# Own-key terms of linear attention from one GpSimd product, and narrow TensorE products in groups of one shape

## The chip, the cores and the metric

One core of a Trainium2 chip runs the whole program. The metric is the device time of one execution in microseconds (us); for the kernel before, the median of three runs is 1870.88 us.

## What is computed

Two transformer blocks over 512 tokens of 1024 channels, in float32. The first block is a token mixer with four groups of heads, and a gated feed-forward layer with a convolution; the second has a short-convolution mixer, a latent attention and two more feed-forward layers. The change lies in the token mixer, in two of its four parts:

- The gated delta rule, four heads of 64 channels. Per chunk of 64 tokens it needs `k k^T` and `q k^T` within the chunk, weighted by decays, the inverse of a unit lower triangular matrix, and the products of that inverse with the values (u) and with the decayed keys (w).
- Linear attention with decays per channel, once as `hg` (four heads of 64 key channels) and once as `gla` (four heads of 32):

```python
a_intra = jnp.einsum('bhnrd,bhnsd,bhnrsd->bhnrs', q, k, jnp.exp(rel))   # s <= r within a block
o_intra = jnp.einsum('bhnrs,bhnse->bhnre', a_intra, v)
```

The term of a token with its own key (r = s) has a decay of 1, so it is the sum over the head's channels of q times k.

## The kernel before, in words

Every product of a weight is made of three float32 matmuls with operands split into high and low parts (`product`, `step`): a column tile of the weight (128 columns) times 512 tokens, eight k tiles deep. Activations are kept as [128 channels, 512 tokens].

The mixer is the first phase (`mix`). `conduct` (L757) writes out the order of TensorE's work by hand. Three lanes hold the mixers as generators: G the gated delta (`gdn`, L1035, two calls of two heads), L the linear attention (`hg` twice with two heads a tile, `gla` once with four heads, all through `la`, L1314), F the forgetting attention. A generator yields the time that the operands of its next products are expected to take; a clock summed from modelled product times decides which lane is due. In between, and at the latest after 1.27 us of lanes' work, one k tile (three matmuls) of a dense product goes into the queue. The dense products are the 29 column tiles of the input weight and, at the end, the 8 of the output weight. Only TensorE's order is fixed so; the other engines' order comes from a scheduler that follows the program's order and the readiness of operands.

Each lane has a ring of PSUM tiles of its own, two deep (`gps`, `lps`, `fps`). Short-lived SBUF tiles of lane L come from the ring `s` of four. `mm` (L703) issues one product, which is two instructions on TensorE for float32 operands; `tr` (L710) a transpose.

In `la`, L1320 to L1334, each head has four products of 128x128 (one a chunk of 128 tokens) of the keys with the queries, on the head's 64 or 32 rows. VectorE multiplies the result by the identity (L1333), which leaves the own-key terms on the diagonal of the tile `lat`; all else in the 128x128 blocks is filled in by seven levels (`la_level`, L1289: a subtraction on GpSimd at L1298, exponentials on ScalarE, products on GpSimd at L1302 and VectorE at L1309). Before that, GpSimd clears the tiles `lbd` (L1322).

In `gdn`, L1075 to L1112, a loop over the two heads makes the gates `e` (in TensorE, then ScalarE), yields, multiplies keys by queries on the head's 64 rows (four products), weights them on VectorE (`weighted`, L1026, four instructions a head), yields, multiplies keys by keys, weights those in place of the gates, and makes from them `mr`, `t1` (mask, L1109) and `xt` (plus identity, L1110). After the loop the values and then both `xt` are transposed (L1115, L1120). At L1164 to L1169 the products of the inverse with the values (`up`: 128x128 weight, 64 columns) and of the keys with the inverse (`wp`: weight of 64 columns, 128 columns moving) alternate, sixteen in all.

Of the kernel before, what the change touches and what calls it, by code (L numbers as in the profile page):

```python
# [9 lines left out]
F32 = mybir.dt.float32  # L10
# [5 lines left out]
ALU = mybir.AluOpType  # L16
AX = mybir.AxisListType

S = 512
# [8 lines left out]
class Builder:  # L28
# [22 lines left out]
    def t(self, shape=(128, S), dt=F32, tag="t", bufs=None, name=None):  # L51
        """A short-lived tile; a lane of the mixer has rings of its own."""
        pool = self.tmp
        if tag in self.lane:
            tag, bufs, own = self.lane[tag]
            pool = self.ph if own else pool
        return pool.tile(list(shape), dt, tag=tag, name=name or tag, bufs=self.rings.get(tag, bufs or 1))
# [12 lines left out]
    def mmt(self):  # L70
        """PSUM of a dense product: two tiles that outlive a phase, or three."""
        self.turn += 1
        if self.turn % self.nmm < 2:
            return self.pmm.tile([128, S], F32, tag="mm", name="mm")
        return self.psm.tile([128, S], F32, tag=self.third, name="mm", bufs=2 if self.third == "pt" else 1)
# [13 lines left out]
    def weight(self, w, ct, kt, between=None, eng=None):  # L89
        """One column tile of a weight: exact high and low parts, [128, kt, 128] in pieces."""  # L90
# [23 lines left out]
    def dense(self, w, ct, xs):  # L114
        """PSUM [128 columns, S tokens] = W[:, ct]^T x, xs a list of (high, low) tiles."""
        return self.product(self.weight(w, ct, len(xs)), xs)
# [14 lines left out]
    def rsqrt_wide(self, ps, scale, tag, n=S):  # L131
        """(mean + eps)^-1/2, with a Newton step, of sums ps (times scale) in PSUM [128, S]."""
# [28 lines left out]
    def stats(self, xs, n, tag):  # L161
        """rows of 1/rms of the tokens on every partition, xs a list of [128, S] tiles."""
# [5 lines left out]
    def gained(self, x, g, tag, bufs=KD):  # L168
        """Exact parts of x times its per-partition gain."""
# [15 lines left out]
    def ready(self, i, ks):  # L185
        """The parts of the x in ks that norm i takes."""
        self.nxt += [self.gained(self.x[k], self.gain(i, k), "x") for k in ks]

    def products(self, w, cts):
        """1 / rms of the tokens, and the products of column tiles with the x of ready()."""  # L190
# [17 lines left out]
    def add_to_x(self, w, xs, gi, n=0):  # L208
        """x += W^T xs, and what the next norm takes of it."""
# [9 lines left out]
    def conv(self, z, y, w, b=None):  # L219
        """y[:, t] = sum_j w[:, j] z[:, t + j] (+ b); z has taps-1 leading zero columns."""  # L220
# [38 lines left out]
    def silu(self, out, z, last=True):  # L259
        """z sigmoid(z); the last of a row brings exp and ln back."""  # L260
# [62 lines left out]
    def final(self, w, xs, gi, out):  # L323
        """The last product and the last norm; the last column tile comes in two halves of the
        tokens, so that the norm of the first runs beside the second."""
# [30 lines left out]
    def write(self, out, half, r):  # L356
        """x times r of one half of the tokens, to DRAM by pairs of tiles."""
# [18 lines left out]
def round_magic(nc, out, in0, scale, shift):  # L376
    """out = nearest integer of in0 * scale + shift."""
# [6 lines left out]
class Mla(Builder):  # L384
# [16 lines left out]
    def rope_tables(self):  # L401
        """cos and signed sin [128, S]; row p serves frequency p % 32."""
# [24 lines left out]
    def swapped(self, raw):  # L427
        """The halves of the rotary columns in each other's place."""
# [20 lines left out]
    def latent(self, cs, g, tag):  # L449
        """Tiles normalised over all their columns, in parts."""  # L450
# [17 lines left out]
    def rotated(self, raw, sw):  # L468
        """The parts of two heads' rotary queries: of the first head the high one over the low
        one, of the second the low one over the high one."""  # L470
# [21 lines left out]
    def mla(self, gi_kv, gi):  # L492
# [15 lines left out]
        # v [tokens, columns] in parts  # L508
# [57 lines left out]
    def scores(self, p, h, b, qn, qr, kn):  # L566
        """Softmax of one head's scores for a block of 128 queries, in rows; gives its last steps."""
# [24 lines left out]
    def attend(self, h, p, vs):  # L592
        """Parts of one head's values weighted by p; a generator that stops after each transpose
        of a block of keys, two blocks ahead of the products."""
# [32 lines left out]
# column tiles of w_in  # L627
# [16 lines left out]
# from a product's end to the next one's start over a step of ScalarE, VectorE, GpSimd (us)  # L644
LA, LV, LP = 0.68, 1.0, 1.5
# the lanes' work between two steps of a dense product, which keep TensorE's clock up (us)
FEED = 1.27
# expected waits (us) on which the order of the lanes' work is set: for a lane's last values, a
# forgetting attention's and a gated delta's inputs, the small gates, 1 / rms, a scaled product,
# a row of silus, the last input of the last products  # L650
# [12 lines left out]
class Mix(Mla):  # L663
    """The mixers' short products run in lanes; a lane is a list of generators that yield
    how long the operands of their next products take. In between go dense products."""

    def mix_consts(self):
# [11 lines left out]
        self.nm1, self.negt = m[:, 0:128], m[:, 128:256]  # L679
        self.resets = c.tile([128, S], BF16, name="resets")  # L680
# [33 lines left out]
    def mm4(self, l, r, cols=lambda t: t):  # L714
        """Block by block l^T r, of some columns."""
# [6 lines left out]
    def stepped(self, ws, xs, tag):  # L722
        """dense(), a generator that stops after each k tile; xs: (k tile, high, low), still
        growing. Yields None where the next is not there yet."""
# [13 lines left out]
    def row_of_out(self, i):  # L738
        """Exact parts of rows of w_out: [128, column tile, 128]."""
# [8 lines left out]
    def idle_psum(self, lanes, live):  # L748
        """PSUM of lanes that have come to their end."""
# [3 lines left out]
    def later(self, gen):  # L753
        """Run gen beside the lane's next task."""
        self.beside.append(Strand(gen, self.clk, self.lane))

    def conduct(self, jobs, lanes):  # L757
        """jobs: (column tile of w_in, task that must be over, name, what to do with the
        product), the urgent first; lanes: lists of (names of inputs, name, generator, rings)."""
# [12 lines left out]
        while True:  # L772
            # what the lanes can start on, and what is due
# [6 lines left out]
            # dense products: evacuate, load the next one's weight  # L780
# [88 lines left out]
    def log1pexp(self, out, z, tmp):  # L869
        """out = ln(1 + exp(-|z|))"""  # L870
# [5 lines left out]
    def rsqrt_small(self, v, n, tag):  # L876
        """v^-1/2 with a Newton step, v an SBUF tile [128, n]."""
# [10 lines left out]
    def to_tokens(self, src, n=4):  # L888
        """PSUM [128 tokens, block, 128 columns] of src [128 columns, tokens]."""
# [5 lines left out]
    def scaled(self, dst, after=None, last=None):  # L895
        """What to do with a product of w_in: times 1 / rms of the tokens, into a new tile."""
# [11 lines left out]
    def silus(self, y, name, last):  # L908
        """silu of y in place, in a row with those that wait if it is the last of the row."""
# [31 lines left out]
    def small(self):  # L941
        """The narrow columns: forget, beta and decay logits, low-rank gate."""
# [3 lines left out]
        # gated delta: [tokens, chunk, head]  # L946
# [30 lines left out]
    def small_fox(self):  # L977
        """Rows 0..3 of a tile: minus the running sum of the log forget gates."""
# [9 lines left out]
    def finish(self, op, pair, gate, g, scale, f=None, dst=None):  # L988
        """RMS over each head of o [tokens, block, 2 heads, 64], gain and gate, in columns."""
# [36 lines left out]
    def weighted(self, out, ps, w, j, e):  # L1026
        """out = ps * e times the row weights w of head j."""
# [7 lines left out]
    def gdn(self, p):  # L1035
# [12 lines left out]
        # sums of squares of the heads, per token  # L1048
# [15 lines left out]
        # 1 / |k|^2 and exp of beta's logarithm less or plus decays  # L1064
# [9 lines left out]
        MT, MR, AT, X, XT = [], [], [], [], []  # L1074
        for j in range(2):  # L1075
            rows = slice(64 * j, 64 * j + 64)
# [9 lines left out]
            for c in range(4):  # L1086
# [3 lines left out]
                )  # L1090
            yield Y_GDN / (1 + j)
            kp = self.pst()
            for c in range(4):
                cs = slice(c * 128, c * 128 + 128)
                self.mm(kp[:, cs], k[rows, cs], q[rows, cs])
            at = self.b("gat", bufs=2)
            self.weighted(at, kp, ik, j, e)
            yield LV
            kp = self.pst()
            for c in range(4):  # L1100
                cs = slice(c * 128, c * 128 + 128)
                self.mm(kp[:, cs], k[rows, cs], k[rows, cs])
            mt = e
            self.weighted(mt, kp, ik, j, e)
# [6 lines left out]
            MT.append(mt), MR.append(mr), AT.append(at), XT.append(xt)  # L1111
            yield LV  # L1112
# [33 lines left out]
        # one refinement: X + X (1 - T X), the defect in float32  # L1146
# [13 lines left out]
        # chunk recurrence  # L1160
# [3 lines left out]
        for c in range(4):  # L1164
            for j in range(2):
                cs = slice(c * 128, c * 128 + 128)
                hs = slice(c * 128 + j * 64, c * 128 + j * 64 + 64)
                self.mm(up[:, hs], XT[j][:, cs], vn[:, hs])
                self.mm(wp[64 * j : 64 * j + 64, cs], ke[:, hs], XT[j][:, cs])  # L1169
# [53 lines left out]
    def hg_bounds(self):  # L1223
        """Lower bounds from a softmax over the one layer, and their logarithms."""
# [17 lines left out]
    def hg_gates(self, p):  # L1242
        """From the forget logits: log forget gates in place, and the keys."""

        def after(f):
# [8 lines left out]
            # logaddexp(ln lb, ln(1 - lb) + f)  # L1254
# [34 lines left out]
    def la_level(self, lv, q, k, g128, g16, es, nh):  # L1289
        """Keys and queries of one level, both decayed to the middles of its blocks."""  # L1290
# [12 lines left out]
        # the heads' queries in blocks of columns of their own  # L1303
# [383 lines left out]
```

## Time and profile before

| | |
|---|---|
| runs | 1869.34, 1870.88, 1871.36 us; median 1870.88 |
| span of the profiled execution | 1867.5 us |
| the profiled execution's own time | not among the numbers at hand; its span is 3.4 us below the median |
| TensorE (PE) busy | 1832.4 us, 98% |
| VectorE (DVE) | 1053.4 us, 56% |
| ScalarE (ACT) | 738.6 us, 40% |
| GpSimd (POOL) | 193.9 us, 10% |
| mixers | from 0 to about 400 us |

The span goes from the first to the last instruction that the profiler records; the time of a run also holds what lies around it. Busy time of TensorE counts pipelined matmuls by their full durations, which overlap: what a product costs the queue is read from the start of one to the start of the next. L numbers are lines of the kernel. A tile's name stands for all its buffers: `lps<-lq,lk` is a product into lane L's PSUM of operands `lq` and `lk`.

### The profile page before, as it was taken

To read this page: it belongs to the slowest core of one execution; us is meant where nothing else is said; L and a number is where in the kernel's file an instruction comes from. 1 tells how busy PE (TensorE), PEld (TensorE's weight loads), DVE (VectorE), ACT (ScalarE), POOL (GpSimd) and SP (SyncE) were. 2 spreads that over 40 slices of the span, in tenths; PEclk is the share of its full clock that TensorE was granted. 3 is DMA by queue.
4 is the path that set the end of the run, shared out by engine and by line. 5 is a ranking of instruction groups with operands and counts; after the bars stand their busy time and mean duration, and the time that the engine had idled before them with its cause. 6 is when DMAs were issued, how large, how long until landed. Compare 5 with 4: busy or idle time off the path is not lost.

```text
span 1867.5 us, 22057 instructions
## 1 busy us (share of the span) xinstructions
PE 1832.4 (98%) x8609; PEld 1502.7 (80%) x8609; DVE 1053.4 (56%) x1627; ACT 738.6 (40%) x1138; POOL 193.9 (10%) x225
## 2 busy tenths in 40 slices
PE   8999999999999999999999999999999999999997
PEld 6787887778888888888888888888777888888886
DVE  7875976767777633455564444334866454444323
ACT  6543534554444422322342332323576433232322
POOL 1510502210000000111200000000111200000001
PEclk9999999999999999999999999999999999999999
DMA  4101111322232333222222223332212222222332
GB/s 166 57 35 46 46 35 35 110 96 97 95 102 91 96 94 97 98 102 91 101 96 102 90 102 99 95 93 97 69 51 74 79 91 102 97 95 97 96 93 76
DMA packets 53223, 162.61 MB, mean 87 GB/s; under 512 B 6528, under 2 KB 13184, under 8 KB 53120
## 3 DMA queue, kind: packets, MB, share of 16 engines
q1 hardware_dynamic: 52992, 161.21, 26.1%
q8 instruction: 67, 1.10, 0.2%
q14 instruction: 36, 0.29, 0.1%
q10 hardware_dynamic: 128, 0.01, 0.0%
HBM read 157.78 MB, written 2.10 MB: 86 GB/s over the span
## 4 chain that ended last, share of the span: by engine, by line
PE 88%; DVE 7%; ACT 2%; issue 1%; POOL 1%; DMA 0%; DVEq 0%; SPq 0%; POOLq 0%; ACTq 0%
PE mm L125 24%; PE mm L127 24%; PE mm L126 24%; PE mm L704 6%; PE gps L704 3%; PE ps L576 2%; PE lps L704 1%; PE fps L704 1%; DVE lbd L1309 1%; DVE lat L1360 1%; DVE wl L112 1%; ACT wh L111 1%; PE pt L605 0%; PE ps L165 0%; POOL s L1298 0%
## 5 line engine op out<-in xcount | busy, mean ns | idle before, releaser
L111 ACT ACTIVATE wh<-raw 128x1024 fp32r<-128x1024 f32 (+3 forms) x308 | 308.7, 1003 | 763.0 <-PE mm L126 463.6
L125 PE MATMUL mm<-xh,wh 128*128 128x512 f32 x1336 | 522.2, 391 | 0.5 <-ACT xh L173 0.5
L126 PE MATMUL mm<-xl,wh 128*128 128x512 f32 x1336 | 521.1, 390 | 0.5 <-DVE xl L174 0.5
L127 PE MATMUL mm<-xh,wl 128*128 128x512 f32 x1336 | 520.3, 389 | 0.0
L112 DVE TENSOR_TENSOR wl<-raw,wh 128x1024 fp32r<-128x1024 f32 (+3 forms) x300 | 362.5, 1208 | 224.7 <-ACT wh L111 221.6
L126 PEld LDWEIGHTS mm<-xl,wh 128*128 128x128 f32 x1336 | 250.9, 188 | 54.5 <-DVE xl L174 1.4
L125 PEld LDWEIGHTS mm<-xh,wh 128*128 128x128 f32 x1336 | 250.9, 188 | 53.6 <-issue 1.0
L127 PEld LDWEIGHTS mm<-xh,wl 128*128 128x128 f32 x1336 | 250.9, 188 | 52.2 <-issue 0.2
L125 PE MATMUL mm<-hidh,wh 128*128 128x512 f32 (+1 forms) x614 | 236.9, 386 | 0.0
L127 PE MATMUL mm<-hidh,wl 128*128 128x512 f32 (+1 forms) x614 | 235.4, 384 | 0.0
L126 PE MATMUL mm<-hidl,wh 128*128 128x512 f32 (+1 forms) x614 | 234.0, 381 | 0.0
L127 PEld LDWEIGHTS mm<-hidh,wl 128*128 128x128 f32 x614 | 115.4, 188 | 24.3
L704 PE MATMUL mm<-xh,wh 128*128 128x512 f32 x291 | 127.7, 439 | 6.8 <-ACT xh L173 5.9
L126 PEld LDWEIGHTS mm<-hidl,wh 128*128 128x128 f32 x614 | 115.5, 188 | 23.4
L125 PEld LDWEIGHTS mm<-hidh,wh 128*128 128x128 f32 x614 | 115.7, 188 | 21.7 <-ACT wh L111 0.2
L704 PE MATMUL mm<-xh,wl 128*128 128x512 f32 x291 | 116.2, 399 | 1.7 <-DVE wl L112 1.7
L704 PE MATMUL mm<-xl,wh 128*128 128x512 f32 x291 | 116.4, 400 | 0.6 <-DVE xl L112 0.4
L278 DVE TENSOR_TENSOR u<-mm,rb 128x512 f32<-128x512 f32 x44 | 30.4, 692 | 141.2 <-PE mm L127 141.2
L158 POOL TENSOR_TENSOR z<-z,sq 128x512 f32<-128x512 f32 x31 | 50.3, 1624 | 558.8 <-ACT sq L156 521.1
L274 DVE TENSOR_TENSOR u<-mm,rb 128x512 f32<-128x512 f32 x44 | 30.4, 691 | 90.9 <-PE mm L127 90.8
L111 ACT ACTIVATE hidh<-s 128x512 fp32r<-128x512 f32 x66 | 41.7, 632 | 88.6 <-DVE s L255 57.5
L704 PEld LDWEIGHTS mm<-xh,wh 128*128 128x128 f32 x291 | 56.1, 193 | 18.8 <-ACT xh L173 6.6
(434 smaller groups left out, 2095.5 us busy)
## 6 DMA issues: line engine op xcount, KB each, us to landing
raw<-in_w_a_dram SPq DMA_DIRECT2D x52, 512.0 KB, 3.3
raw<-in_w_b_dram SPq DMA_DIRECT2D x52, 512.0 KB, 3.3
raw<-in_w_up_dram SPq DMA_DIRECT2D x44, 512.0 KB, 3.2
raw<-in_w_in_dram SPq DMA_DIRECT2D x28, 512.0 KB, 3.2
raw<-in_conv_w_in_dram SPq DMA_DIRECT2D x24, 512.0 KB, 3.2
raw<-in_w_down_dram SPq DMA_DIRECT2D x16, 448.0 KB, 3.2
raw<-in_w_a_dram SPq DMA_DIRECT2D x16, 448.0 KB, 3.3
raw<-in_w_b_dram SPq DMA_DIRECT2D x16, 448.0 KB, 3.3
```

The source lines that it names most:

```text
L111: nc.scalar.activation(out=h, in_=src, func=ACTF.Copy)
L112: (eng or nc.vector).tensor_tensor(out=l, in0=src, in1=h.bitcast(F32), op=ALU.subtract)
L125: nc.tensor.matmul(out=ps, lhsT=h, rhs=xh, start=(k == 0), stop=False)
L126: nc.tensor.matmul(out=ps, lhsT=h, rhs=xl, start=False, stop=False)
L127: nc.tensor.matmul(out=ps, lhsT=l, rhs=xh, start=False, stop=(k == kt - 1))
L158: eng.tensor_tensor(out=acc, in0=acc, in1=sq, op=ALU.add)
L274: nc.vector.tensor_tensor(out=g, in0=ps, in1=r, op=ALU.mult)
L278: nc.vector.tensor_tensor(out=g, in0=ps, in1=r, op=ALU.mult)
L576: nc.tensor.matmul(out=ps[:, :n], lhsT=l[:, qs], rhs=r[:, :n], start=(i == 0), stop=False)
L704: self.nc.tensor.matmul(out=out, lhsT=lhsT, rhs=rhs, start=start, stop=stop)
L1309: nc.vector.tensor_tensor(out=bd[rows, :, h].rearrange("p c (n j) -> p c n j", j=b), in0=c4(q)[rows], in1=c4(d)[rows], op=ALU.mult)
L1360: nc.vector.copy_predicated(out=at.rearrange("p c (n j) -> p c n j", j=2 * b)[:, :, :, b:], mask=self.lmask[:, lv - 1].rearrange("p (n j) ...
```

## The change

In the constants, one column of ones per head:

```diff
+        self.heads = {}
+        for nh in (2, 4):
+            self.heads[nh] = c.tile([128, nh], F32, name=f"heads{nh}")
+            nc.vector.tensor_reduce(
+                out=self.heads[nh], in_=self.ident.rearrange("p (h d) -> p h d", h=nh), axis=AX.X, op=ALU.add
+            )
```

In `la`, queries times keys are formed once on GpSimd, and four products with the head columns (weight: 128 channels by 128 tokens; moving: 2 or 4 columns) sum them over each head's channels. VectorE multiplies the identity by the column of sums:

```diff
+        own = self.t(tag="s", bufs=3)
+        nc.gpsimd.tensor_tensor(out=own, in0=q, in1=k, op=ALU.mult)
+        yield LP
+        kp = self.pst()
+        for c in range(4):
+            self.mm(kp[:, c * nh : c * nh + nh], own[:, c * 128 : c * 128 + 128], self.heads[nh])
+        kp = kp[:, : 4 * nh].rearrange("p (c h) -> p c h", h=nh)
         for h in range(nh):
-            rows = slice(h * dk, h * dk + dk)
-            yield LV
-            kp = self.pst()
-            for c in range(4):
-                cs = slice(c * 128, c * 128 + 128)
-                self.mm(kp[:, cs], k[rows, cs], q[rows, cs])
             at = self.b("lat", bufs=4)
-            nc.vector.tensor_tensor(out=c4(at), in0=c4(kp), in1=idb, op=ALU.mult)
+            nc.vector.tensor_tensor(
+                out=c4(at), in0=idb, in1=kp[:, :, h].unsqueeze(2).to_broadcast([128, 4, 128]), op=ALU.mult
+            )
             AT.append(at)
```

In `gdn`, the gates of both heads come first, then both heads' keys with queries in one group that alternates between the heads' rows, then both heads' keys with keys:

```diff
+            E.append(e)
             yield Y_GDN / (1 + j)
-            kp = self.pst()
+
+        def keys_with(r):
+            kp = [self.pst() for _ in range(2)]
             for c in range(4):
                 cs = slice(c * 128, c * 128 + 128)
-                self.mm(kp[:, cs], k[rows, cs], q[rows, cs])
+                for j in range(2):
+                    rows = slice(64 * j, 64 * j + 64)
+                    self.mm(kp[j][:, cs], k[rows, cs], r[rows, cs])
+            return kp
+
+        for j, kp in enumerate(keys_with(q)):
             at = self.b("gat", bufs=2)
-            self.weighted(at, kp, ik, j, e)
-            yield LV
-            kp = self.pst()
-            for c in range(4):
-                cs = slice(c * 128, c * 128 + 128)
-                self.mm(kp[:, cs], k[rows, cs], k[rows, cs])
-            mt = e
-            self.weighted(mt, kp, ik, j, e)
+            self.weighted(at, kp, ik, j, E[j])
+            AT.append(at)
+        yield 2 * LV
+        for j, kp in enumerate(keys_with(k)):
+            mt = E[j]
+            self.weighted(mt, kp, ik, j, mt)
             mr = self.b("gmr", F32R, bufs=2)
...
-            MT.append(mt), MR.append(mr), AT.append(at), XT.append(xt)
-            yield LV
+            MT.append(mt), MR.append(mr), XT.append(xt)
+        yield LV
```

and the products with the inverse are issued as all of `up`, then all of `wp`:

```diff
-        for c in range(4):
-            for j in range(2):
-                cs = slice(c * 128, c * 128 + 128)
-                hs = slice(c * 128 + j * 64, c * 128 + j * 64 + 64)
-                self.mm(up[:, hs], XT[j][:, cs], vn[:, hs])
-                self.mm(wp[64 * j : 64 * j + 64, cs], ke[:, hs], XT[j][:, cs])
+        blocks = [
+            (slice(c * 128, c * 128 + 128), slice(c * 128 + j * 64, c * 128 + j * 64 + 64), j)
+            for c in range(4) for j in range(2)
+        ]
+        for cs, hs, j in blocks:
+            self.mm(up[:, hs], XT[j][:, cs], vn[:, hs])
+        for cs, hs, j in blocks:
+            self.mm(wp[64 * j : 64 * j + 64, cs], ke[:, hs], XT[j][:, cs])
```

The constants on which `conduct` sets the order (LA, LV, LP, Y_GDN and the others) stay. The diff also drops comments, which changes no instruction.

## Rows read from the trace of the kernel before

**Rows 1.** The page: its first line, and the busy time of TensorE.
```profile
span 1867.5 us, 22057 instructions
...
PE 1832.4 (98%) x8609; PEld 1502.7 (80%) x8609; DVE 1053.4 (56%) x1627; ACT 738.6 (40%) x1138; POOL 193.9 (10%) x225
```

**Rows 2.** Busy time by stretch: length, each engine (instructions), clock, DMA share, GB/s.
```profile
175.00:200.00 25.00, 24.75 (x122) 18.94 (x121) 19.01 (x33) 12.24 (x23) 7.05 (x6) 1.00 0.18 64
200.00:225.00 25.00, 24.81 (x135) 20.05 (x134) 22.40 (x62) 16.69 (x38) 13.21 (x12) 1.00 0.12 43
225.00:250.00 25.00, 23.55 (x137) 20.10 (x135) 21.77 (x62) 7.14 (x8) 5.43 (x6) 1.00 0.13 43
...
0.00:400.00 400.00, 378.45 (x2094) 310.74 (x2094) 294.31 (x629) 194.63 (x380) 98.38 (x110) 0.99 0.20 68
```

**Rows 3.** Timeline of TensorE about one narrow group of gdn: start us, us, instruction.
```profile
57.76 0.39 PE L704 MATMUL mm<-xh,wl 128*128 128x512 f32 x1
58.08 1.16 PE L704 MATMUL gps<-gq,gk 64*128 64x128 f32 x8
...
59.50 0.39 PE L704 MATMUL mm<-xl,wh 128*128 128x512 f32 x1
59.73 0.40 PE L704 MATMUL mm<-xh,wl 128*128 128x512 f32 x1
```

**Rows 4.** Instructions of line 704, the narrow groups: min/median/max ns, first and last start.
```profile
L704 PE MATMUL lps<-lq,lk x64: 269/272/374, 65.9 to 321.7; 64*128 64x128 f32 x32, 32*128 32x128 f32 x32
...
L704 PE MATMUL gps<-gq,gk x32: 271/272/374, 58.1 to 220.6; 64*128 64x128 f32 x32
```

**Rows 5.** Timeline of TensorE about products with 16 columns, in the small gates.
```profile
33.27 0.29 PE L704 MATMUL gps<-gg,mixc 128*128 128x16 f32 x2
33.40 0.38 PE L704 MATMUL gps<-gg,ones 128*128 128x16 f32 x2
33.63 0.49 PE L704 MATMUL mm<-xh,wh 128*128 128x512 f32 x1
33.95 0.40 PE L704 MATMUL mm<-xl,wh 128*128 128x512 f32 x1
```

**Rows 6.** VectorE in la: own-key products, and the levels' block products (min/median/max ns).
```profile
L1333 DVE TENSOR_TENSOR lat<-lps,mlac x8: 664/692/692, 69.7 to 322.0; 128x512 f32<-128x512 f32 x8
...
L1309 DVE TENSOR_TENSOR lbd<-lq,s x56: 401/422/1440, 65.6 to 353.1; 64x256 f32<-64x256 f32 x28, 32x256 f32<-32x256 f32 x28
```

**Rows 7.** GpSimd: a product of [128, 512], and its idle time before two calls' first subtraction.
```profile
L1374 POOL TENSOR_TENSOR lqi<-lq,lqi x3: 1273/1589/2084, 66.3 to 296.4; 128x512 f32<-128x512 f32 x3
...
58.50 3.05 POOL L1298 TENSOR_TENSOR s<-lg 128x512 f32<-128x512 f32 x2 [5.34 <-DVE gkof L1070]
...
186.95 4.20 POOL L1298 TENSOR_TENSOR s<-lg 128x512 f32<-128x512 f32 x3 [18.75 <-DVE lg L1337]
```

**Rows 8.** Timeline of TensorE: start of sixteen alternating pairs, and the dense step after.
```profile
150.34 0.33 PE L704 MATMUL gps<-gvn,gmr 128*128 128x64 f32 x2
...
156.05 0.50 PE L704 MATMUL mm<-xh,wh 128*128 128x512 f32 x1
```

**Rows 9.** Timeline: second head's keys to its transpose on TensorE, and VectorE between.
```profile
72.16 1.16 PE L704 MATMUL gps<-gk 64*128 64x128 f32 x8
...
78.40 0.60 PE L711 MATMUL gps<-mlac,gxt 128*128 128x128 f32 x4
...
73.92 1.12 DVE L1030 SCALAR_TENSOR_TENSOR gmt<-gps,gik,gmt 128x128 f32<-128x128 f32 x4
...
77.28 0.69 DVE L1110 TENSOR_TENSOR gxt<-u,mlac 128x512 fp32r<-128x512 f32 x1
```

**Rows 10.** Busy time by stretch, before a fall of the clock, and two of the falls.
```profile
107.50:110.90 3.40, 2.06 (x13) 1.48 (x12) 3.38 (x8) 0.00 (x0) 0.00 (x0) 1.00 0.00 0
111.00:114.30 3.30, 3.30 (x11) 2.82 (x10) 3.27 (x6) 1.78 (x2) 0.00 (x0) 0.50 0.00 0
...
295.40:298.70 3.30, 3.30 (x13) 2.42 (x12) 3.29 (x4) 3.26 (x6) 2.01 (x2) 0.50 0.23 73
```

More of the change, by code (lines that the diff above doesn't have):

```diff
@@ L1074, in gdn @@
         MT, MR, AT, X, XT = [], [], [], [], []
+        E = []
         for j in range(2):
-            rows = slice(64 * j, 64 * j + 64)
             gp = self.pst()
```

## The prediction

> **What bounds the kernel now.** I read the page first. TensorE is busy 98% of the span [rows 1], and the change touches only the token mixers, which fill the first 400 us. In them TensorE is busy 378.45 us of 400 [rows 2], so 21.55 us are all that any wait can have there; lanes of short products and dense products lie in one fixed order in TensorE's queue, and after the lanes end dense products still follow. Time taken out of TensorE's queue should therefore come out of the total, unless TensorE then waits for another engine. The engine to watch is VectorE: from 175 to 250 us, where gated delta and linear attention run together, it is busy 19.01, 22.40 and 21.77 us of 25 each [rows 2].
>
> The unit of every sum is the step from the start of one instruction to the start of the next, because the durations overlap. Dense steps are 0.23 us apart (59.50 to 59.73). A float32 product of 128x128 is two instructions. A group of four on 64 rows stands alone between the dense starts at 57.76 and 59.50 [rows 3]. That is 1.74 us; without the group there would be two dense steps, 0.46, so the group costs 1.28 us. Between its first instruction (58.08) and the dense one after it lie eight steps, about 0.11 each or 0.89 in all; the remaining 0.39 is paid on entering and leaving the shape of 64 rows.
>
> **Own-key terms (la).** Removed: 64 instructions, half on 64 and half on 32 rows, that is 8 groups of eight [rows 4], 8 x 1.28 = 10.2 us. Added: in each of three calls four products of a 128x128 weight with 2 or 4 columns, eight instructions. The nearest rows have 16 columns: four instructions from 33.27 to the second dense start after them at 33.95, less one dense step, make 0.68 - 0.23 = 0.45, or 0.112 each [rows 5]. So few columns do not make a step shorter; eight cost 0.90, three calls 2.7. Net -7.5 us. I take the bounds as equal to it, since 16 columns already stand at the floor that 128 columns show.
>
> VectorE still makes one [128, 512] product a head: 8 x 0.69 us as before [rows 6]; the operand in PSUM becomes a repeated column, which I cost at no difference. GpSimd gets three products of [128, 512], 1.27 to 2.08 us each, 1.59 in the middle [rows 7]. They are hidden: GpSimd sat idle 5.34 us before the first level's subtraction of the first call, and 18.75 us before that of the second [rows 7], and by the order of the code queries and keys are there before the summed decays that the subtraction needs. If that cover is gone, the subtractions of the levels queue behind the product and TensorE's queue stands at the sum over heads, up to 2.08 us a call and 0.5 for the hand-over, 7.8 us in all (bounds 0 and 7.8, taken 0). The two reductions that make the head columns run once among the loads at the start; I take 0.
>
> **Keys with queries, keys with keys (gdn).** Removed: 32 instructions of keys with queries [rows 4] and, by the code, as many of keys with keys, 8 groups of eight, 8 x 1.28 = 10.2 us. Added: four groups of sixteen, in which the halves of the rows alternate. No row shows two halves following each other. If a step stays 0.111, a group costs 16 x 0.111 + 0.39 = 2.17 us, four 8.7: -1.6 us, only the four entries saved. If the halves run side by side, eight steps of time remain, 1.28 a group: -5.1 us. The nearest row is of 64 rows, but always of the same half, so it excludes neither; I take the middle, -3.3.
>
> The Trainium skill (TensorEngine Tiling, Key Properties) states that different tiles of the array can load weights and multiply in parallel. By that rule this term is -5.1 and the whole sum 1.8 us lower than mine.
>
> **Values and keys by the inverse (up, wp).** Before, pairs of the full shape and of 64 columns alternate, sixteen pairs, 32 instructions from 150.34 to 156.05, 5.71 us, and once more in the other call [rows 8]. That is 0.178 a step against 0.111 within one shape. After: two blocks of sixteen with one change of shape between and one behind, 32 x 0.111 + 0.3 = 3.9 us. Two calls: -3.7 us. Were the 64-column halves to run side by side, the second block would take half: 3.0 us, -5.4 in two calls. Here I take the row's step, -3.7.
>
> Sum on TensorE: -7.5 - 3.3 - 3.7 = -14.5 us, between -12.8 and -18.0.
>
> **New waits.** In gdn both heads' weighting now follows one group of products. VectorE's part for one head is four products by gates (1.12 us for the four), the mask product and the identity sum (0.69 each): 2.5 us [rows 9]. Two heads are 5.0. Before, the first head's part ran while the second head's gates were made. TensorE comes to the last transpose of that inverse 6.24 us after the start of the last keys' group (72.16 to 78.40) [rows 9], and now 0.9 us later, the group being twice as long: 7.1. Needed are about 1.9 for the group, 5.0 for VectorE and the foreign work on VectorE that stands between: from 73.92 to the end of the identity sum at 77.97 it took 4.05 us for its 2.5 [rows 9], so 1.55. That makes 8.45, and a wait of 1.35 us a call, with all other lanes' products queued behind; two calls +2.7 (bounds 0 and 5.0 a call, all of VectorE's two heads exposed, 10.0).
>
> From 175 to 250 us VectorE has 75 - 63.2 = 11.8 us to spare [rows 2], and the changes take 4 x 1.28 - 0.9 (the call with four heads) + 1.6 (one gdn call) = 5.8 us of TensorE's time out of that stretch, which would leave VectorE busy 91% of the rest; I take 1 us lost there (0 to 5.8). The granted clock stood at 0.50 for 3.3 us from 111.0, after a stretch in which TensorE was busy 2.06 us of 3.40 [rows 10]; such a fall costs about half its length, 1.6 us, and another stands at 295.4 us [rows 10]. Other gaps will move them: 0, with one fall, 1.6 us, to either side.
>
> **Sum**: -14.5 + 2.7 + 1.0 = -10.8 us. The profiled span is 1867.5 [rows 1], 3.4 below the median of the runs, 1870.88; what lies around the span is not touched. So the span should be 1856.7 and the time 1860.1 us.
>
> **Rivals.** *The halves run side by side*, of rows and of columns: -18.0 + 3.7 = -14.3, 1856.6 us. For it: separate PSUM tiles and separate rows; against: weights are loaded every 0.11 us whatever the shape in all rows. 0.25.
>
> *VectorE becomes the bound* in the stretches where gdn and la overlap. For it: 22.40 of 25 there. Then the 5.8 us of that stretch are not won: -14.5 + 2.7 + 5.8 = -6.0, 1864.9. Against: TensorE's own busy time in the same stretch is higher still. One more thing speaks for it: VectorE's block products take 0.42 us in the middle but 1.44 at the worst [rows 6]; if that is GpSimd's work beside it, three more products can cost VectorE about 1 us each, 1867.9 in all. 0.20.
>
> The Trainium skill (GPSIMD Engine Reference, Key points) states that GpSimd shares its SBUF interfaces with VectorE and contends with its instructions of two SBUF inputs. By that rule the 1867.9 would hold; the spread of [rows 6] is in line with it, though those rows don't show what GpSimd did at the time.
>
> *The product on GpSimd is late*, so that own-key terms are not cheaper at all: 7.8 us of waits at the sum over heads, 1860.1 + 7.8 = 1867.9. Against: the idle time in [rows 7]. 0.08.
>
> *Slower*: in gdn TensorE stands at the transposes until VectorE has done both heads. Only two PSUM buffers serve that lane, so that each group waits for the weighting of the one before. It decides when none of the 2 x 1.1 us of the first weighting and none of the 5.0 us lies beside other work: 7.2 us a call, and a fall of the clock by 1.6 behind each gap. With TensorE's saving at its lower bound that is -12.8 + 2 x 8.8 = +4.8, 1875.7 us. It turns slower from 6.4 us of gap and fall a call. Against: dense steps stand between these groups, and their time is cover. 0.06.
>
> **How the numbers follow.** My forecast has the remaining 0.41. About 0.2% of the time, 3.7 us, can be told from no change, so faster means under 1867.1. All of the forecast but a few hundredths, the side-by-side case and somewhat more than half of VectorE's case are faster: 0.79; the rest of that case and the late product give 0.14 the same; slower 0.07. The range goes from 1852 (side by side, little waiting and one clock fall fewer: 1870.88 - 18.0 - 1.6 + 1) to 1868 (VectorE's case at its worst), leaving out the slower rival; it also holds the forecast with all of VectorE's two heads exposed, 1860.1 + 10.0 - 2.7 = 1867.4.
>
> **What would show it.** Right: instructions of 64 and 32 rows gone from la; three short groups of 2 or 4 columns at 0.11 a step without a wait ahead; in gdn groups of sixteen, whose step (0.11 or 0.055) settles the middle term; two blocks instead of sixteen pairs, 3.9 us long; lanes and dense products ending some 10 us earlier, and everything behind 400 us unchanged. A wait of 1 to 2 us at the transposes behind the keys' products, ended by VectorE, is expected. Wrong: TensorE's idle time in the mixers growing by more than 5 us, waits ended by GpSimd at the sums over heads, or more time at a clock of 0.50 than the stage's mean of 0.99 leaves room for [rows 2].

## The result, and the profile after

The kernel after takes 1891.7 us (median of four runs, 1884.84 to 1893.5) against 1870.7 us for the kernel before: a ratio of 1.011, 95% interval 1.0095 to 1.0126. It is slower by 21 us, where 10.8 us less were forecast. The profiled execution took 1893.5 us with a span of 1891.7, that is 24.2 more than before [rows 1].

The page of the kernel after: span, busy time, and the granted clock of TensorE in 40 slices.

```profile
span 1891.7 us, 21988 instructions
...
PE 1831.4 (97%) x8569; PEld 1504.8 (80%) x8569; DVE 1057.5 (56%) x1629; ACT 740.0 (39%) x1138; POOL 194.7 (10%) x228
...
PEclk9989998999999999999999999999999999999999
```

TensorE has 40 instructions fewer and almost the same busy time as in [rows 1]; part of its work must have run slower. The stretches of [rows 2] in the kernel after, with the same columns:

```profile
175.00:200.00 25.00, 24.74 (x127) 20.02 (x127) 16.68 (x34) 11.55 (x23) 3.74 (x3) 1.00 0.13 43
200.00:225.00 25.00, 16.87 (x79) 13.91 (x78) 19.37 (x39) 15.96 (x36) 14.04 (x12) 0.86 0.13 43
225.00:250.00 25.00, 20.58 (x124) 16.27 (x123) 23.91 (x69) 7.90 (x15) 9.36 (x8) 1.00 0.13 43
...
0.00:400.00 400.00, 353.00 (x1958) 293.81 (x1959) 287.54 (x619) 185.03 (x364) 89.39 (x106) 0.94 0.19 63
```

In the first 400 us TensorE is idle 47.0 us instead of 21.55, and its mean clock is 0.94 instead of 0.99. The mixers end (start of the first dense product behind them, line 125) at 421.6 us instead of 399.9: all of the loss but 2.5 us is there.

**The changed products do what was forecast.** TensorE's timeline of the kernel after, at an own-key group, a group of keys with queries, and the products of the inverse:

```profile
66.51 0.95 PE L711 MATMUL lps<-heads,s 128*128 128x2 f32 x8
67.31 0.48 PE L711 MATMUL mm<-xh,wh 128*128 128x512 f32 x1
...
160.18 1.89 PE L711 MATMUL gps<-gvn,gmr 128*128 128x64 f32 x16
162.00 1.09 PE L711 MATMUL gps<-gmr,gke 128*64 128x128 f32 x16
163.02 0.50 PE L711 MATMUL mm<-xh,wh 128*128 128x512 f32 x1
...
227.55 1.21 PE L711 MATMUL gps<-gq,gk 64*128 64x128 f32 x16 [0.66 <-ACT gmt L1094]
228.69 0.50 PE L711 MATMUL mm<-xh,wh 128*128 128x512 f32 x1
```

The group of eight of the kernel before [rows 3], and the dense instruction behind it:

```profile
58.08 1.16 PE L704 MATMUL gps<-gq,gk 64*128 64x128 f32 x8
59.16 0.50 PE L704 MATMUL mm<-xh,wh 128*128 128x512 f32 x1
```

Eight own-key instructions take 0.80 us to the next start. Sixteen of alternating row halves take 1.14 us, where eight on one half took 1.08 (58.08 to 59.16): a group of sixteen costs about what one of eight did, so halves of rows run side by side. The blocks of `up` and `wp` take 1.82 and 1.02 us, 2.84 where the pairs took 5.71 [rows 8], so halves of columns do so too. By these rows the instructions got cheaper by 7.5 (own keys), 5.1 (four groups less of 1.28) and 5.7 us (2 x 2.87): **18.3 us**. That is the better bound of each term of the prediction, and 0.3 us past it for `up` and `wp`.

**Where more than that went.** Waits of TensorE in the first 420 us of the kernel after, by releaser: total us, times, longest.

```profile
PE mm L711 <- ACT xh L173: 7.2, 1, 7.2
PE lps L711 <- DVE lst L1418: 4.0, 1, 4.0
PE gps L711 <- DVE gxt L1156: 4.0, 1, 4.0
PE gps L711 <- ACT gko L1068: 3.3, 2, 2.3
PE lps L711 <- DVE lat L1380: 3.2, 1, 3.2
PE gps L718 <- ACT gq L261: 2.9, 1, 2.9
PE lps L711 <- DVE lbd L1325: 2.9, 1, 2.9
PE gps L711 <- DVE gat L1037: 2.2, 2, 2.0
...
PE gps L711 <- ACT gmt L1094: 2.0, 2, 1.3
...
PE gps L718 <- DVE gmt L1037: 1.4, 2, 0.9
```

The first is the kernel's start. It was 5.9 us before, and in runs with the same start it is 6.0 (`abc_same`, `after_waits`), so its 1.3 us belong to this execution and not to the change. Only `gat` and `gmt` at L711, 4.2 us together, stand at groups that the change made, and `gmt` at L718 (1.4) at the transposes behind them; the others are in linear attention's states and levels, in the gated delta's later steps and at silus. Ten waits are of 1.8 us or more; the kernel before has one such, at its start. The largest behind the start, and what follows it (TensorE, then VectorE):

```profile
116.91 0.39 PE L711 MATMUL lps<-lv,lko 128*128 128x128 f32 x2
121.27 0.71 PE L711 MATMUL lps<-lst,lqi 128*128 128x128 f32 x2 [3.97 <-DVE lst L1418]
...
124.76 0.63 PE L711 MATMUL mm<-xl,wh 128*128 128x512 f32 x1
125.19 0.63 PE L711 MATMUL mm<-xh,wl 128*128 128x512 f32 x1
...
117.88 1.50 DVE L1461 SCALAR_TENSOR_TENSOR fk<-rk,mixp,sq 64x512 f32<-64x512 f32 x2
...
120.98 0.23 DVE L1418 COPY lst<-lps 64x64 f32<-64x64 f32 x1
```

The copy that TensorE needs takes 0.23 us, but stands on VectorE behind forgetting attention's keys and a convolution. Behind the wait the granted clock is 0.50 for 17.1 us: dense steps are 0.43 us apart (124.76 to 125.19) instead of 0.23. In the trace's record of the clock, TensorE is at that lower level for 44.4 us of the mixers (six falls, from 70.2, 121.4, 213.6, 288.6, 316.0 and 370.6 us) and 6.8 us more at 1381 us; before it was three falls, 10.2 us in all.

The three amounts close: -18.3 for instructions, +25.45 idle, and, as an estimate of what the clock cost, half of the added low-clock time, (44.4 + 6.8 - 10.2) / 2 = +20.5, make +27.7 against 24.2 measured. (A last stretch at the lower level, 11 us at the end of the span, is in every run and left out.)

### The profile page after: what moved, and what is told of

Same layout as the page of the kernel before. It is cut to its first block, busy times and chain, and to the rows that moved or that the text cites. A ratio compares the mean times of both kernels' runs of the same rounds, so it can differ in the third digit from the quotient of the medians.

```text
span 1891.7 us, 21988 instructions
## 1 busy us (share of the span) xinstructions
PE 1831.4 (97%) x8569; PEld 1504.8 (80%) x8569; DVE 1057.5 (56%) x1629; ACT 740.0 (39%) x1138; POOL 194.7 (10%) x228
## 4 chain that ended last, share of the span: by engine, by line
PE 88%; DVE 6%; ACT 3%; issue 1%; DMA 1%; POOL 0%; SPq 0%; DVEq 0%; POOLq 0%; ACTq 0%
PE mm L125 24%; PE mm L127 24%; PE mm L126 24%; PE mm L711 7%; PE gps L711 3%; PE ps L576 2%; PE lps L711 1%; PE fps L711 1%; DVE lbd L1325 1%; DVE wl L112 1%; ACT wh L111 1%; PE pt L605 0%; DVE lat L1380 0%; PE ps L165 0%; ACT L261 0%
## 5 line engine op out<-in xcount | busy, mean ns | idle before, releaser
L711 PE MATMUL mm<-xh,wh 128*128 128x512 f32 x292 | 130.4, 446 | 8.0 <-ACT xh L173 7.2
L711 PE MATMUL mm<-xh,wl 128*128 128x512 f32 x292 | 118.7, 406 | 1.9 <-DVE wl L112 1.9
L711 PE MATMUL mm<-xl,wh 128*128 128x512 f32 x292 | 118.4, 405 | 0.1
L711 PEld LDWEIGHTS mm<-xh,wh 128*128 128x128 f32 x292 | 57.9, 198 | 19.6 <-ACT xh L173 7.4
```

The costliest lines, as they stand in the source:

```text
L711: self.nc.tensor.matmul(out=out, lhsT=lhsT, rhs=rhs, start=start, stop=stop)
```

## The experiments

Two theories were set against each other. **Order**: the products are cheaper, but moving the yields changes TensorE's whole written-out order in the mixers, and this order no longer meets those of VectorE, ScalarE and GpSimd. **Structure**: the new products themselves wait longer, since both heads stand behind one group or GpSimd's product. In the expectations order is theory 1. Structure is theory 3 where it means the gated delta's two heads behind one group; theory 2 is that the new instructions themselves cost, by GpSimd's product or by falls of the clock. Ratios are to the kernel before, run beside each, with 95% intervals; they differ by up to 0.2% from the quotients of the medians.

Whether an edit kept the order can be read from the traces. Leave out the changed products and compare, by tile names, the first 2000 instructions of TensorE with those of the kernel before. None is out of sequence in `c_alone`, `a_same`, `a_same_c`, `b_same` and `abc_same`; 34 are in `n_feed`, 137 in `n_gdn`, 223 in `a_order` and in `a_alone`, 344 in the kernel after and 355 in `after_waits`.

### Each part by itself

`c_alone` makes only the edit of `up` and `wp`. `a_alone` makes only the change in `la`, as the diff has it. `b_alone` makes only the change of the two keys' groups in `gdn`. `a_same` has the instructions of `a_alone`, but the planner is told nothing new: the yields and modelled times are the old ones, so everything else keeps its place in TensorE's queue (its edit against `a_alone`):

```diff
-        yield LP
-        kp = self.pst()
...
         for h in range(nh):
+            yield LV
+            was = self.clk
+            if h == 0:
+                kp = self.pst()
...
+            self.clk = was + 4 * 1.69e-3 * 128
```

> The kernel before with only the regrouped up and wp products; the order of everything else in TensorE's queue is the same. Theory 1 (the time is lost to the new order of TensorE's queue, the products themselves got cheaper): 2.87 us saved in each of two calls, 5.7 us in all, 1865 us, with at most the three falls of the clock that the kernel before had. Theory 2 (the cheaper, narrower groups themselves let the clock fall): a fall follows the shorter blocks, 1868 to 1875 us.

> Own-key terms by the GpSimd product and the sums over heads, but with the places of the old products kept in the planner's clock, so that TensorE's queue has the order of the kernel before, less the narrow groups. Theory 1 (order): 7.5 us saved, 1863 us, waits of TensorE as before (21 us idle in the first 400 us). Theory 2 (the new instructions themselves, GpSimd's product beside VectorE or too little work for the clock): waits or falls of the clock grow here too, 1875 us or more.

> The same own-key terms as in the change, with one pause in the place of one for each head, so that the planner sets another order; gated delta as before. Theory 1 (order): loses the 7.5 us of the run with the order kept and more, 1872 to 1885 us, with more idle time of TensorE at places that have nothing to do with the own-key terms. Theory 3 (the gated delta's two heads in one group are what costs): 1863 us, as with the order kept.

> Only the gated delta's keys with queries and keys with keys in groups of both heads, gates first. Theory 1 (order): 5 us saved on the products, given back by another order, 1870 to 1885 us. Theory 3 (waits on VectorE for both heads, and a fall of the clock behind each, are what costs): 1880 to 1890 us with the waits at the keys' groups and the transposes behind them, and little elsewhere.

Measured: `c_alone` 1864.4 us, 0.9974 (0.996 to 0.9988); `a_same` 1866.87, 0.9983 (0.9973 to 0.9992); `a_alone` 1889.93, 1.0109 (1.0094 to 1.0124); `b_alone` 1902.65, 1.0188 (1.0153 to 1.0223). The same own-key instructions gain 4 us in the old order and lose 19 in the new one. The parts are not additive: `a_alone` and `b_alone` lose 19 and 32 us, the whole change 21. Of the expectations only that of `c_alone` was met, by theory 1: `a_same` gained 4 of the 7.5 us, and `a_alone` and `b_alone` came out slower than any theory had them. Theory 2 is out for these products: in the old order neither `c_alone` nor `a_same` loses time.

### Order without the instructions

`a_order` undoes the other half: the old products, per head on 64 or 32 rows, in the places that `a_alone` gives the new ones. `n_gdn` and `n_feed` are the kernel before with one constant of the plan moved; no instruction changes, only the order of TensorE's queue and, through the scheduler, that of the other engines.

```diff
-Y_FIN, Y_FOX, Y_GDN, Y_SM = 8.3, 8.64, 4.0, 5.33
+Y_FIN, Y_FOX, Y_GDN, Y_SM = 8.3, 8.64, 4.5, 5.33
```

```diff
-FEED = 1.27
+FEED = 1.4
```

> The old own-key products (four of 128x128 for each head), issued in one group after one pause and charged to the planner's clock as the new ones are, so that TensorE's queue has the order of the run a_alone without its new instructions. Theory 1 (the order is what costs): 7.5 us above a_alone, 1895 to 1900 us. Theory 2 (the new instructions cost): near the kernel before, 1868 to 1878 us.

> The kernel before with one constant of the planner changed: the wait that it expects for the gates of the gated delta from 4.0 to 4.5 us. No instruction is added or removed, some 70 places in TensorE's queue are exchanged. If any other order costs (the old one fits the other engines by its constants): 1876 to 1890 us, with new waits and falls of the clock. If orders differ little and it is what the change does in it that costs: 1868 to 1873 us.

> A second change of order without any change of instructions: the kernel before with the planner's bound on the lanes' work between two dense steps at 1.40 instead of 1.27 us. If any other order costs: 1874 to 1886 us. If the run with the gates' wait was an unlucky one: 1867 to 1873 us.

Measured: `a_order` 1883.29 us, 1.0078 (1.0059 to 1.0096); `n_gdn` 1883.43, 1.0065 (1.0043 to 1.0087); `n_feed` 1871.94, 1.0013 (1.0003 to 1.0024). The stretch of the mixers in `a_order`, and its two largest waits of TensorE behind the first 40 us:

```profile
0.00:400.00 400.00, 365.19 (x2013) 300.43 (x2014) 288.88 (x619) 185.62 (x365) 89.54 (x103) 0.97 0.20 65
...
PE gps L704 <- DVE gy L1136: 4.8, 1, 4.8
PE gps L704 <- DVE gxt L1142: 3.1, 3, 2.2
```

TensorE is idle 34.81 us with the old products, 13.3 more than before, and the largest waits stand in the gated delta's later steps, which this run does not touch; its own-key products wait 0.8 us in all. Order alone thus costs up to 0.8%. `n_feed` hardly costs anything, but it also moves few instructions. By these runs the plan's order is the cause, not TensorE's queue by itself: the other engines' orders move with it, and no run separates them.

`n_gdn` came out as theory 1 had it, `n_feed` not. `a_order` met neither of its two: theory 1 had it 7.5 us above `a_alone`, and it is 5 us nearer to the kernel before (14 us above it, `a_alone` 19). TensorE's sequence is the same in both, so in this order the cheaper own-key products did not gain their 7.5 us but lost some 5. The accounts below put this down to idle time and the clock; why they grow is open.

### Cheaper products in the old order

`a_same_c` joins `a_same` and `c_alone`. `b_same` issues the groups of both heads at the second head's old places; `abc_same` has all three parts in the old order.

```diff
...
+            was = self.clk
+            if j == 1:
+                for i, kp in enumerate(keys_with(q)):
+                    at = self.b("gat", bufs=2)
+                    self.weighted(at, kp, ik, i, E[i])
+                    AT.append(at)
+            self.clk = was + 4 * 1.69e-3 * 128
             yield LV
...
```

> The two parts that leave TensorE's order as it was: own-key terms with the old places, and up and wp in blocks. Theory 1: the savings add, 13 us on the products and about what a_same lost to waits and clock back, 1859 to 1863 us, faster than both kernels.

> The gated delta's two grouped products alone, with their places in the planner kept: the queue has the order of the kernel before, both heads' products standing where the second head's stood. This isolates what the groups save (10.2 - 5.1 us on the products) and the wait for VectorE's two heads behind them, which the prediction set at 1.35 us a call. Theory 1 (order): 1866 to 1871 us, faster than before by what is left of 5.1 after waits of 1 to 3 us a call. Theory 3 (VectorE's two heads behind one group are what makes the change slow): waits of 4 us and more a call and falls of the clock, 1876 us or more.

> Every new instruction of the change, in the order of the kernel before (all places in the planner kept). Theory 1 (order): 18 us saved on TensorE's products less 5 to 10 us of waits that come back, 1858 to 1866 us, some 28 us below the change itself. Theory 3: 1872 us or more.

Measured: `a_same_c` 1863.55 us, 0.9967 (0.9955 to 0.9978); `b_same` 1876.95, 1.0033 (1.002 to 1.0046); `abc_same` 1868.02, 0.9996 (0.9985 to 1.0006). `a_same_c` beats both kernels. All of the change's instructions in TensorE's old order are 1.1% (21 us) faster than the kernel after, by the ratios, but no faster than the kernel before: the groups of `gdn` take back what the other two parts gain. `a_same_c` came out where theory 1 had it, within 0.6 us; `b_same` where theory 3 had it; `abc_same` between the two. Why, `abc_same` shows on ScalarE and TensorE:

```profile
68.81 0.42 ACT L1319 ACTIVATE s<-s 128x256 f32<-128x256 f32 x1 [2.31 <-POOL s L1318]
...
69.44 1.12 ACT L1103 ACTIVATE gmt<-gps,gbias 128x128 f32<-128x128 f32 x4
```

```profile
65.69 0.48 PE L710 MATMUL gps<-gq,gk 64*128 64x128 f32 x2
70.61 1.65 PE L710 MATMUL gps<-gq,gk 64*128 64x128 f32 x12 [4.44 <-ACT gmt L1103]
```

The second head's gates (1.12 us on ScalarE) stand behind an exponential that waits 2.31 us for GpSimd's subtraction. All of TensorE's group but its first product must wait until the second head's gates have freed their PSUM tile (the ring has two), so the first head, ready earlier, waits too: 4.44 us, and from 69.3 us on the clock is at its lower level for 6.8 us. This is the structure theory, true for this part.

### Longer waits in the plan

The other way to mend the order: keep the new groups, and tell the planner how long their operands take. `b_waits` does it to `b_alone`, `after_waits` to the whole change.

```diff
-            yield Y_GDN / (1 + j)
+            yield Y_GDN
...
-        yield 2 * LV
+        yield 3.5 * LV
```

> The gated delta's part alone, as b_alone, with the planner's waits lengthened to what b_alone's trace shows: 4.0 us for the second head's gates too (was 2.0) and 3.5 instead of 2.0 between the two groups. Theory 3 (b_alone's own waits at those groups and the falls behind them cost 12 of its 32 us): 1885 to 1892 us. If the rest of the order decides: anywhere from 1870 to 1905 us, with the waits at the groups gone all the same.

> The whole change, with the planner told longer waits in the gated delta: 4.0 us ahead of the keys' products for both heads' gates and 3.5 us between the two groups of products, the constants that took 12.7 us off the gated delta's part alone (1902.65 to 1889.97 us). If the change loses its time because two constants of the plan are too short for the new groups, the same 10 to 13 us come back: 1879 to 1882 us, TensorE idle under 40 us of the first 400 (47.0 in the change) with the waits at the keys' groups and transposes gone. If the loss comes from the whole written-out order meeting the other engines' queues elsewhere, another order is only another draw: 1880 to 1900 us, idle 38 to 50 us, the waits of 2 to 4 us at other places, and above the kernel before in any case.

Measured: `b_waits` 1889.97 us, 1.0103 (1.0079 to 1.0128); `after_waits` 1874.97, 1.0033 (1.0016 to 1.0049). `b_waits` fits both of its expectations. In the change two constants bring back some 0.77%, 14.4 us by the ratios, and the run is faster than both of its expectations had it (1879 and more), so its time does not decide between them. What the constants do can be seen at one place. TensorE in the kernel after:

```profile
64.62 1.16 PE L711 MATMUL gps<-gq,gk 64*128 64x128 f32 x14 [1.34 <-ACT gmt L1094]
...
67.86 0.40 PE L711 MATMUL mm<-xh,wl 128*128 128x512 f32 x1
70.23 0.79 PE L711 MATMUL gps<-gk 64*128 64x128 f32 x2 [1.98 <-DVE gat L1037]
71.27 2.07 PE L711 MATMUL gps<-gk 64*128 64x128 f32 x14 [0.24 <-DVE gat L1037]
73.27 0.79 PE L711 MATMUL mm<-xh,wh 128*128 128x512 f32 x1
```

and in `after_waits`, with the first 400 us behind it:

```profile
64.43 1.16 PE L711 MATMUL gps<-gq,gk 64*128 64x128 f32 x16
...
69.55 0.39 PE L711 MATMUL mm<-xh,wl 128*128 128x512 f32 x1
70.23 0.49 PE L711 MATMUL gps<-gk 64*128 64x128 f32 x2 [0.29 <-DVE gat L1037]
71.26 1.16 PE L711 MATMUL gps<-gk 64*128 64x128 f32 x14 [0.55 <-DVE gat L1037]
72.35 0.50 PE L711 MATMUL mm<-xh,wh 128*128 128x512 f32 x1
```

```profile
0.00:400.00 400.00, 361.04 (x2027) 299.62 (x2028) 291.89 (x628) 191.48 (x372) 100.48 (x112) 0.97 0.20 66
```

The keys' group starts at 70.23 us in both, because VectorE's weighting is no earlier. In `after_waits` dense steps stand in the time that the kernel after stood idle, and the group then runs at full speed (1.16 us) instead of half (2.07). Elsewhere waits remain, 2.9 us at the transposes among them, and TensorE is idle 38.96 us in all: two constants are not a plan tuned anew.

### The accounts of all runs

From each profiled execution, against the kernel before, in us: the instructions by the rows above, idle time of the first 400 us, half of the low-clock time (whole span), their sum, and the span. (Where the mixers go on behind 400 us, the idle time there is not in it.)

| run | instructions | idle | half of low clock | sum | span |
|---|---|---|---|---|---|
| `c_alone` | -5.7 | +2.7 | -5.1 | -8.1 | -9.2 |
| `a_same` | -7.5 | +3.8 | +3.4 | -0.3 | +0.4 |
| `a_same_c` | -13.2 | +5.7 | +5.1 | -2.4 | -2.8 |
| `abc_same` | -18.3 | +12.4 | +1.7 | -4.2 | -1.9 |
| `after_waits` | -18.3 | +17.4 | +6.8 | +5.9 | +4.8 |
| `b_same` | -5.1 | +7.4 | +5.1 | +7.4 | +8.4 |
| `n_feed` | 0 | +0.4 | 0 | +0.4 | +2.6 |
| `n_gdn` | 0 | +5.9 | +10.2 | +16.2 | +16.3 |
| `a_order` | 0 | +13.3 | +6.8 | +20.1 | +16.7 |
| `a_alone` | -7.5 | +16.5 | +15.4 | +24.4 | +22.0 |
| the kernel after | -18.3 | +25.5 | +20.5 | +27.7 | +24.2 |
| `b_alone` | -5.1 | +16.9 | +15.4 | +27.2 | +30.2 |
| `b_waits` | -5.1 | +15.8 | +22.2 | +32.9 | +30.6 |

The sums meet the spans within 3.5 us, and one profiled run can differ from its kernel's median by as much as a fall or two of the clock: `b_waits` ran from 1885.89 to 1899.9 us, and the profiled run was the longest; `c_alone`'s, without a fall in the mixers, was the shortest of eight. Even in the old order cheaper products leave more idle time (`a_same` 3.8 us, `c_alone` 2.7). A likely reason is that these products also covered the time in which the lanes' operands were made; no run here shows that by itself.

## Why the prediction was wrong

- **The terms on TensorE were right**, at their better bound: -18.3 us measured where -14.5 (to -18.0) stood. The values taken for the gated delta's groups (-3.3, by the rows -5.1) and for `up` and `wp` (-3.7, by the rows -5.7) were too small; side by side was the case in both. The rule of the Trainium skill (TensorEngine Tiling, Key Properties) that different tiles work in parallel agrees with this trace: sixteen instructions in 1.14 us. A reading that changes no term: from the first of eight instructions to the dense one behind them it is 1.08 us, not 0.89; the 1.28 us of the whole group stand.
- **The step that failed** is the first inference: "Time taken out of TensorE's queue should therefore come out of the total, unless TensorE then waits for another engine." The "unless" was priced only at the gated delta's groups (+2.7) and in one stretch of VectorE (+1.0). Idle time grew by 25.45 us, most of it at products that the change does not touch; growth by more than 5 us was named as what would prove the forecast wrong. The prediction had TensorE's work in one fixed order and took that order as unchanged around the edits, though they move the yields from which `conduct` makes it. What the runs showed in its place: the change's instructions in the old order take the time of the kernel before (`abc_same`, 0.9996), in the order that the edits make 1.011. `a_order` loses 0.78% with no new instruction; `after_waits` gets 0.77% back from two constants.
- **The clock** was put at 0 with 1.6 to either side, one fall. By the estimate above it cost 20.5 us, since waits of some 2 to 4 us, of which the new order has many, are often followed by a fall.
- **Waits in the gated delta** were the right mechanism. The forecast had 1.35 us a call at the last transpose. The kernel after has 1.34 and 1.98 us at the groups themselves and a fall behind; with the order kept it is 4.44 at the group, in one call. What was missed is ScalarE's queue, in which the second head's gates stand behind linear attention's exponentials.
- **VectorE as the bound** was not the cause: until the mixers end it is busy 300.4 of 421.6 us, against 294.2 of 399.9 before, a smaller share. It is late at single places, because its queue holds other things first.
- **GpSimd** costs TensorE nothing at the sum over heads: in the kernel after the own-key groups have no wait ahead of them (the one at 66.51 us above).
- **The slower rival** had its sign right and its place wrong: it asked for 6.4 us a call at the transposes. It would have had to be "the fixed order no longer fits", priced by the idle time that a plan not tuned to the new pieces leaves, over all 400 us.

## What to carry to other kernels

Where an in-order queue is written out by a planner with tuned constants, an edit to a yield can move every later place in that queue, and with it the other engines' orders. Cost it by a run that moves only the order, and try new instructions first in the old order, as `a_same_c` did (0.9967): here order was worth about 1.1%, and the instructions gained a third of that at best. Merging two heads' products into one group makes the earlier head wait for the later; give the group its slot by the later head's operands, and look for them in the queues of every engine that makes them.

## What the hardware showed that was not expected

- Float32 products on different halves of rows, or of columns, run side by side: 16 instructions in 1.14 and 1.02 us, against eight in 1.08 on one half of the rows alone.
- Of the six falls of the clock in the mixers of the kernel after, five began within 1 us of the end of a wait of 1.8 to 4 us, and one inside such a wait; two such waits, which end at 204.9 and 249.2 us, had no fall behind them. The three falls of the kernel before stand behind waits of 0.4 to 1.0 us. The six lasted 3.4 to 17.1 us. With the one at 1381 us, and at half their length, they cost 20.5 us more than those three, nearly as much as the added idle time of 25.45.
- VectorE slows beside GpSimd. Here are, of the kernel after, VectorE's block products and what GpSimd did meanwhile:

```profile
64.56 4.46 DVE L1325 TENSOR_TENSOR lbd<-lq,s 64x256 f32<-64x256 f32 x4
```

```profile
65.19 1.26 POOL L1314 TENSOR_TENSOR s<-lg 128x512 f32<-128x512 f32 x1
66.41 1.47 POOL L1394 TENSOR_TENSOR lqi<-lq,lqi 128x512 f32<-128x512 f32 x1
67.83 0.91 POOL L1318 TENSOR_TENSOR lw<-lk,s 128x256 f32<-128x256 f32 x1
```

Four take 4.46 us, 1.1 each, where the middle one took 0.42 [rows 6]: what the prediction only suspected. Of the 28 such products of 64x256 in this trace, the 14 that had GpSimd busy for less than a tenth of their time took 0.41 to 0.42 us, the four that had it busy for more than four fifths 0.85 to 1.39. That agrees with the Trainium skill (GPSIMD Engine Reference, Key points), by which the two share their SBUF interfaces and contend where VectorE's instruction has two inputs there. The kernel before has it too (0.95 to 1.42 us at the same four products), but there the first head's weighting stands ahead of them; here it stands behind them and is late, and TensorE stood for it at 70.23 us. The same happens in `after_waits` without harm, because dense steps cover it.
